# Products with low weights moved to the end of each projection's half in a hybrid decoder layer, with a new order of all work

## Chip, cores and metric

The kernel runs on one core of one Trainium2 chip. The metric is device time in microseconds for one call, the median of several runs. TensorE (PE) does the matrix products, VectorE (DVE) and ScalarE (ACT) the elementwise work, GpSimd (POOL) issues the accumulating transfers, and SyncE (SP) all other transfers.

## What is computed

One decoder layer for 1024 tokens of width 1024, all in float32. Attention (16 query heads, 4 key heads, head size 64) mixes three dilated windows; beside it stands a causal convolution over 31 tokens, followed by a layer norm. Both branches are gated, and one output projection brings them together.

```python
h = rmsnorm(x, norm_g)
proj = einsum('bsd,de->bse', h, w_in)            # 1024 -> 5632 columns
q, k, v, a_gate, c_val, c_glu, c_gate = split(proj)
y_att = attention_branch(q, k, v, a_gate)        # windows (128,1) (512,4) (2048,16)
y_conv = conv_branch(c_val, c_glu, c_gate, conv_w, conv_b, ln_g, ln_b)
x = x + einsum('bse,ed->bsd', concat([y_att, y_conv]), w_out)
return rmsnorm(x, final_norm_g)
```

## The kernel before

**Products in pieces.** PE takes its operands in a rounded 32-bit form, so each float32 matrix is split into a high part (a rounded copy) and a low part (the rest), and a product A·W is three: high·high, low·high and high·low. For the in-projection (`inproj`, L637) the pieces are `hhi`, `hlo` (normed input, one pair per half of the tokens) and `wh`, `wl` (128 columns of the weights, loaded as `raw`). There are 44 such column blocks; each has two halves of 512 tokens, and each half takes 24 products in one PSUM bank, named `ps`. In this document a block is named by its first column: ps2304 is the block at column 2304, ps2304_0 its first half.

**Weights.** For 40 of the 44 blocks `split_dma` makes the pieces: SP loads `raw`, ACT writes `wh` and then minus `wh` into `wl`, and a transfer issued by POOL adds `raw` into `wl` (`add_into`, L297). So `wl` is complete one transfer later than `wh`. For the first two blocks and for those with the last gates DVE subtracts instead.

**Attention.** `attend(p)` handles one pair of heads (p = 0 to 7). It takes scores in units: six far units (two named far0, far1, far3 for each head), which use `qf` and cover the dilated windows, then a small round trip through DRAM, then eight near units (near0 to near6 for each head), which use `qs`. Each unit is a few small products on PE into one of two score banks, then one or more `add_min` on DVE (L283, it adds the bias table and takes the minimum) and an exponential on ACT (L251). A bank is free for the next unit but one only when DVE has read it. Then follow transposes (`tp`), products with the values (`on`, `of`), a transfer of the result to `y` by POOL, the gate on DVE (`y<-y,ag`, L268) and a store to `y_dram`. The query projection also writes `qs` by DVE (L268) and `qf` by ACT.

**Convolution.** `convolve(p)` is 46 multiply-adds on DVE per block (L268, buffers `c`, `t`, `hc`), which are spread over the same stretch as the attention of pair p.

**End.** After the last pair come a layer norm of the convolution's result in two halves (`cc`, `mean`, `var`, `lst`, `rb`: PE sums, DVE finishes, PE spreads `rb` over the partitions), the output projection of the attention (`opsa`, eight row blocks, low pieces of the input `yla`), and that of the convolution (`opsc`, low pieces `ylc`).

**Who sets the order.** The functions above only record operations in a `Plan`: engine, modelled cost, inputs and outputs. `Plan.order` then simulates all engines and picks for each the operation that can start first, with a priority that is the place in the recorded order less a boost (`TUNE`: `w` loads and splits of weights, `use` what reads a projection's bank, `ln`, `att`, `conv`, `ap` and `wo` the streams of that name). `LIMITS` caps how many buffers of a kind are alive at once, and `SECTIONS` lists which projections run beside which pair (`h4` is a convolution block's two projections, `q3` a query block, `a2` a gate). What comes out is pinned: each engine's instructions and each queue's transfers run strictly in that order. So one changed line in `inproj` or one changed number can move work everywhere.

Of the kernel before, what the change touches and what calls it, by code (L numbers as in the profile page):

```python
# [19 lines left out]
ND = D // P  # L20
# [11 lines left out]

LIMITS = {"x": 5, "raw": 2, "raw_oc": 1, "raw_oa": 2, "wh": 3, "wl": 3, "tab": 1, "e": 7, "pt": 4, "vs": 4, "vc":
          4, "turn": 2, "opsa": 2, "score": 2, "hc": 5, "c": 7, "t": 1, "g": 1, "gl": 7, "y": 2, "ag": 4, "cc": 5,
          "qs": 5, "qf": 4, "kdh": 9, "kdl": 5, "yc": 1, "ya": 2, "zc": 7, "za": 3}

RESERVE = {"e": 7, "pt": 3}
BANKS = {"mm": 3, "sc": 2, "tp": 2, "o": 1}  # L40
WARM = 55
LATE = C_CG + 6 * P
MORE = (10, 12)
TUNE = {"w": 225, "use": 260, "ln": 65, "att": 240, "conv": -15, "wo": 185, "woa": 20, "ap": 0, "wait": 0.2116}
SECTIONS = [("k0 q0 h1 v", 0), ("h2 a0 q1", 1), ("h3 a1 q2", 1), ("a2 q3 h4", 1), ("h5 k1 a3 q4", 1), ("h6 a4 q5",
            1), ("c0 h7 a5 q6 c1 q7", 1), ("a6 a7 c2 c3", 1), ("c4 c5", 1), ("c6 c7", 0)]


# [113 lines left out]
class Plan:  # L162
# [140 lines left out]
    def order(self):  # L303
# [55 lines left out]
        while len(out) < n:  # L359
            best = None  # L360
            for e, todo in ready.items():
                now, pick = None, None
                for i in sorted(todo, key=self.prio.__getitem__):
                    t = start_of(i)
                    if t is None:
                        continue
                    soon = t - TUNE["wait"] if self.prio[i] < i - 300 else t
                    if now is None or soon < now - 1e-9:
# [94 lines left out]
def layer_kernel(tc, x, norm_g, w_in, conv_w, conv_b, ln_g, ln_b, w_out, fin_g, tab, out):  # L463
# [3 lines left out]
    def pool(name, space=None):  # L467
# [4 lines left out]
    pl = Plan(tc, {  # L472
        "big": (sb, "big", 4), "c8": (sb, "c8", 1), "c4": (sb, "c4", 33), "c2": (sb, "c2", 5), "st": (sb, "st", 16),
        "sx": (sb, "sx", 6),
        **{k: (ps, k, BANKS[k]) for k in PSUM_KINDS},
    }, LIMITS)

# [34 lines left out]
    def c4(shape, name, dtype=F32):  # L512
        group = name.rstrip("0123456789_")
        return pl.buf("c4", shape, dtype, name, group=group if group in pl.limits else None)

    def bank(kind, name, group=None):
        return pl.buf(kind, [P, 512], F32, name, group=group)
# [24 lines left out]
    hhi = [pl.buf("big", [P, ND, 512], F32R, f"hhi{i}") for i in range(2)]  # L542
    hlo = [pl.buf("big", [P, ND, 512], F32R, f"hlo{i}") for i in range(2)]
# [9 lines left out]
    raw, ready = {}, {}  # L553
# [68 lines left out]
    def load_raw(col):  # L622
        raw = c4([P, ND, P], f"raw{col}")
        pl.load(raw, w_in[:, col:col + P].rearrange("(c p) n -> p c n", p=P))
        return raw

    def split_w(col, raw, split=split_dma):
        wh, wl = c4([P, ND, P], f"wh{col}", F32R), c4([P, ND, P], f"wl{col}", F32R)
        split(wh, wl, raw)
        return wh, wl  # L630

    def load_w(col):
        if col in ready:
            return ready[col]
        old, pl.boost = pl.boost, TUNE["w"]
        w = split_w(col, load_raw(col), split_r if col >= LATE else split_dma)
        pl.boost = old  # L637
        return w

    def inproj(col, use, cuts=((0, 512), (0, 512))):  # L640
        wh, wl = load_w(col)
        for half in range(2):
            b = bank("mm", f"ps{col}_{half}")
            for n0, n1 in zip(cuts[half], cuts[half][1:]):
                if n0:
                    yield 0.5
                for c in range(ND):
                    pl.mm([(b[:, n0:n1], wh[:, c, :], hhi[half][:, c, n0:n1], c == 0, False),
                           (b[:, n0:n1], wh[:, c, :], hlo[half][:, c, n0:n1], False, False),
                           (b[:, n0:n1], wl[:, c, :], hhi[half][:, c, n0:n1], False, c == ND - 1)])  # L650
            pl.boost = TUNE["use"]
            use(half, b, slice(half * 512, half * 512 + 512))
            pl.boost = 0
            yield 1.0
# [3 lines left out]
    vs = [c4([P, 2, NKV, P], f"vs{i}", F32R) for i in range(4)]  # L658
    vc = [c4([P, 2, NKV, P], f"vc{i}", F32R) for i in range(4)]
# [4 lines left out]
    def project_v():  # L664
        for n in range(2):
            vt, vn = c4([P, 4, 256], f"vt{n}"), c4([P, 8, 4, 32], f"vn{n}")

            def use(half, b, cs):
                pl.act(rest(vt, half), b.fourth(), AF.Copy)
                pl.act(vn[:, 4 * half:4 * half + 4], b.blocks(), AF.Copy)  # L670
            yield from inproj(C_V + n * P, use)
            for g in range(4):
                for name, to in (("n", vs), ("f", vc)):
                    b = bank("tp", f"vT{n}_{name}{g}")
                    src = [vn[:, i].flat() if name == "n" else vt[:, g, (i % 2) * P:(i % 2) * P + P]
                           for i in (2 * g, 2 * g + 1)]
                    pl.mm([(b[:, j * P:(j + 1) * P], src[j], ident, None, None) for j in range(2)])
                    both = to[g][:, :, 2 * n:2 * n + 2, :]
                    split_r(both[:, :, :, 0:DH], both[:, :, :, DH:P],
                            b[:, 0:256].shaped("p (j k d) -> p j k d", 2, 2, DH, j=2, k=2))  # L680
# [3 lines left out]
    def project_k(kc):  # L684
        for kv in (2 * kc, 2 * kc + 1):
            kd[kv] = (c4([P, 4, 256], f"kdh{kv}", F32R), c4([P, 4, 256], f"kdl{kv}", F32R))

        def use(half, b, cs):
            for j in range(2):
                kh, kl = kd[2 * kc + j]  # L690
                r, o = slice(j * DH, j * DH + DH), slice((1 - j) * DH, (1 - j) * DH + DH)
                h, l, src = rest(kh, half), rest(kl, half), b[r, :].fourth()
                pl.act(h[r], src, AF.Copy)
                pl.act(h[o], src, AF.Copy)
                pl.tt(l[r], src, h[r].cast(F32), ALU.subtract)
                pl.act(l[o], l[r].cast(F32), AF.Copy)
        yield from inproj(C_K + kc * P, use)

    qs, qf = {}, {}

    def project_q(p):
        for j in range(2):
            qs[2 * p + j] = c4([P, S], f"qs{2 * p + j}", F32R)
            qf[2 * p + j] = c4([P, 2, 4, P], f"qf{2 * p + j}", F32R)

        def use(half, b, cs):
            for j in range(2):
                q = qs[2 * p + j]
                r, o = slice(j * DH, j * DH + DH), slice((1 - j) * DH, (1 - j) * DH + DH)
                pl.act(q[r, cs], b[r, :], AF.Copy, scale=-(DH ** -0.5))  # L710
                pl.stt(q[o, cs], b[r, :], -(DH ** -0.5), q[r, cs].cast(F32), ALU.mult, ALU.subtract)
                pl.act(qf[2 * p + j][:, half], q[:, cs].fourth().cast(F32), AF.Copy)
        yield from inproj(C_Q + p * P, use)
# [6 lines left out]
    ag = {}  # L720
# [15 lines left out]
    hc = {}  # L736
# [361 lines left out]
    def boosted(name, gen):  # L1098
        while True:
            pl.boost = TUNE[name]  # L1100
            w = next(gen, None)
            pl.boost = 0
            if w is None:
                return
            yield w

    def section(k, weight, spine, more=()):
        nonlocal done
        proj, m = SECTIONS[k]
        hs = [boosted("att", attend(i)) for i in range(done, done + m)]  # L1110
# [48 lines left out]
```

## Time and profile before

| | us |
|---|---|
| median of 3 runs (909.42 to 910.8) | 910.27 |
| the profiled execution's own time | 910.03 |
| its span, first to last instruction | 908.2 |
| PE busy | 875.1 (96%) |
| DVE busy | 656.1 (72%) |
| ACT busy | 591.3 (65%) |
| POOL busy | 53.3 (6%) |

The span is what the trace covers; 1.8 us of the profiled execution's time lie around it. Three views are used below. The view of waits lists how long an engine stood before an instruction and what it stood for. The view of windows gives, for a stretch of time, each engine's busy time and PEclk, the share of full speed that the TensorE clock was granted. The timeline gives single instructions with their start.

### The profile page before, as it was taken

How to read it: one execution, taken by the hardware profiler on the slowest of the kernel's cores; microseconds unless marked ns; L12 is line 12 of the kernel's file. 1: busy time of each engine (PE TensorE's matmuls, PEld its weight loads, DVE VectorE, ACT ScalarE, POOL GpSimd, SP SyncE). 2: the span in 40 equal slices, each digit the busy share in tenths (PEclk: the TensorE clock that was granted, in tenths of full speed). 3: DMA queues.
4: the chain of work that ended last, by engine and by line, in shares of the span. 5: the costliest groups of instructions: out<-in, count | busy, mean ns of one | idle time of the engine just before them, and what ended most of it. 6: DMA issues, size and time to landing. Idle time of an engine off the chain costs nothing. (4 is left out here: it accounts for less than half of the span.)

```text
span 908.2 us, 13036 instructions
## 1 busy us (share of the span) xinstructions
PE 875.1 (96%) x4493; PEld 731.2 (81%) x4493; DVE 656.1 (72%) x1506; ACT 591.3 (65%) x1392; POOL 53.3 (6%) x69
## 2 busy tenths in 40 slices
PE   8999999999999999999998998899999899999996
PEld 7888888878888888878886887688887678778885
DVE  5769995798699699989587658874659895615432
ACT  5777469387979889678786764795796754404111
POOL 0011001101010110100011000001000000000000
PEclk9999999999999999999999999699999999999999
DMA  7653306436353673464357323366765697758211
GB/s 259 186 119 67 96 3 140 93 91 144 70 118 59 163 165 83 93 135 101 96 128 173 70 70 92 73 152 132 206 201 194 186 372 255 252 177 239 93 47 47
DMA packets 104953, 123.53 MB, mean 136 GB/s; under 512 B 17941, under 2 KB 78357, under 8 KB 104888
## 3 DMA queue, kind: packets, MB, share of 16 engines
q1 hardware_dynamic: 97000, 94.40, 33.6%
q0 software_dynamic: 7888, 28.32, 17.2%
q8 instruction: 35, 0.57, 0.3%
q14 instruction: 30, 0.25, 0.1%
HBM read 65.35 MB, written 24.84 MB: 99 GB/s over the span
## 5 line engine op out<-in xcount | busy, mean ns | idle before, releaser
L236 PE MATMUL ps<-hhi,wh 128*128 128x512 f32 (+1 forms) x720 | 291.1, 404 | 0.2 <-ACT hhi L249 0.2
L236 PE MATMUL ps<-hhi,wl 128*128 128x512 f32 (+1 forms) x720 | 282.3, 392 | 6.1 <-DMA wl<-raw 4.8
L236 PE MATMUL ps<-hlo,wh 128*128 128x512 f32 (+1 forms) x720 | 281.8, 391 | 0.4 <-DVE hlo L264 0.3
L236 PEld LDWEIGHTS ps<-hhi,wl 128*128 128x128 f32 x720 | 136.6, 190 | 38.2 <-DMA wl<-raw 6.5
L236 PEld LDWEIGHTS ps<-hlo,wh 128*128 128x128 f32 x720 | 137.2, 191 | 23.8 <-DVE hlo L264 1.0
L236 PEld LDWEIGHTS ps<-hhi,wh 128*128 128x128 f32 x720 | 137.0, 190 | 23.0 <-issue 0.5
L251 ACT ACTIVATE e<-e,near 128x256 f32<-128x256 f32 (+1 forms) x256 | 115.0, 489 | 17.4 <-DVE near L264 11.5
L268 DVE SCALAR_TENSOR_TENSOR c<-t,taps,c 128x511 f32<-128x511 f32 (+14 forms) x120 | 88.5, 737 | 0.0
L268 DVE SCALAR_TENSOR_TENSOR c<-hc,taps,c 128x511 f32<-128x511 f32 (+14 forms) x120 | 88.2, 735 | 0.3
L268 DVE SCALAR_TENSOR_TENSOR t<-hc,taps,t 128x511 f32<-128x511 f32 (+6 forms) x112 | 82.6, 738 | 0.3 <-ACT t L251 0.2
L236 PE MATMUL opsc<-woc,yhc 128*128 128x512 f32 (+1 forms) x272 | 81.0, 381 | 0.0
L251 ACT ACTIVATE e<-e,far 128x96 f32<-128x96 f32 (+1 forms) x128 | 53.8, 423 | 25.9 <-DVE far L283 25.2
L297 POOL DMA_DIRECT2D wl<-raw x40 | 34.9, 873 | 414.2 <-ACT wl L251 315.5
L236 PEld LDWEIGHTS opsc<-woc,yhc 128*128 128x128 f32 x272 | 50.1, 188 | 10.7
L236 PE MATMUL opsc<-woc,ylc 128*128 128x512 f32 (+1 forms) x136 | 52.0, 383 | 1.4 <-DVE ylc L264 1.4
L251 ACT ACTIVATE fjunk<-zc 128x512 bf16<-128x512 f32 (+1 forms) x17 | 10.3, 606 | 62.2 <-DVE zc L264 62.2
L236 PE MATMUL opsa<-woah,yla 128*128 128x512 f32 x112 | 45.0, 402 | 2.6 <-DVE yla L264 2.6
L249 ACT CAST wh<-raw 128x1024 fp32r<-128x1024 f32 x44 | 46.0, 1046 | 0.4 <-DMA raw<-in_w_in 0.4
L236 PE MATMUL opsa<-woah,yha 128*128 128x512 f32 x112 | 45.6, 408 | 0.4 <-DVE cc L264 0.4
L236 PE MATMUL opsa<-woal,yha 128*128 128x512 f32 x112 | 45.1, 402 | 0.0
L251 ACT ACTIVATE e<-e,f 128x224 f32<-128x224 f32 (+1 forms) x128 | 45.0, 436 | 0.0
L249 ACT CAST qf<-qs 128x512 fp32r<-128x512 f32 x32 | 34.3, 1120 | 13.5 <-DVE qs L268 13.5
(176 smaller groups left out, 1525.2 us busy)
## 6 DMA issues: line engine op xcount, KB each, us to landing
raw<-in_w_in SPq DMA_DIRECT2D x44, 512.0 KB, 5.4
wl<-raw POOLq DMA_DIRECT2D x40, 512.0 KB, 4.7
x<-in_x SPq DMA_DIRECT2D x8, 512.0 KB, 10.2
tab<-in_tab SPq DMA_DIRECT2D x8, 512.0 KB, 3.8
c_dram<-c SPq DMA_DIRECT2D x8, 512.0 KB, 2.7
g_dram<-g SPq DMA_DIRECT2D x8, 512.0 KB, 3.1
raw_oa<-in_w_out SPq DMA_DIRECT2D x8, 512.0 KB, 5.1
raw_oc<-in_w_out SPq DMA_DIRECT2D x8, 512.0 KB, 7.9
```

The source lines that it names most:

```text
L236: nc.tensor.matmul(out.ap(), a.ap(), b.ap(), start=start, stop=stop)
L249: nc.scalar.copy(out.ap(), x.ap())
L251: nc.scalar.activation(out.ap(), x.ap(), func, **{k: ap_of(v) for k, v in kw.items()})
L268: lambda: self.nc.vector.scalar_tensor_tensor(out.ap(), a.ap(), ap_of(s), b.ap(), op0, op1),
L297: self.op("POOL", 1.0, lambda: self.nc.gpsimd.dma_start(ap_of(dst), x.ap(), accum_op=ALU.add), [dst], [x, dst])
```

## The change

In `inproj` the 24 products of a half are issued in another order. Before: eight times (high input with high weights, low input with high weights, high input with low weights). Now: eight times the first two, 16 products in all, then the 8 products with low weights in four operations of two. The products are the same and their number too. The buffer limits (`wl`, `hc`, `c`, `gl` and `za` one more; `y`, `qs` and `kdh` one fewer), six boosts, and the place of the gate projection `a2` change with it, and the order of all engines comes out anew.

```diff
--- before.py
+++ after.py
@@ -32,17 +32,17 @@
 
 
 
-LIMITS = {"x": 5, "raw": 2, "raw_oc": 1, "raw_oa": 2, "wh": 3, "wl": 3, "tab": 1, "e": 7, "pt": 4, "vs": 4, "vc":
-          4, "turn": 2, "opsa": 2, "score": 2, "hc": 5, "c": 7, "t": 1, "g": 1, "gl": 7, "y": 2, "ag": 4, "cc": 5,
-          "qs": 5, "qf": 4, "kdh": 9, "kdl": 5, "yc": 1, "ya": 2, "zc": 7, "za": 3}
+LIMITS = {"x": 5, "raw": 2, "raw_oc": 1, "raw_oa": 2, "wh": 3, "wl": 4, "tab": 1, "e": 7, "pt": 4, "vs": 4, "vc":
+          4, "turn": 2, "opsa": 2, "score": 2, "hc": 6, "c": 8, "t": 1, "g": 1, "gl": 8, "y": 1, "ag": 4, "cc": 5,
+          "qs": 4, "qf": 4, "kdh": 8, "kdl": 5, "yc": 1, "ya": 2, "zc": 7, "za": 4}
 
 RESERVE = {"e": 7, "pt": 3}
 BANKS = {"mm": 3, "sc": 2, "tp": 2, "o": 1}
 WARM = 55
 LATE = C_CG + 6 * P
 MORE = (10, 12)
-TUNE = {"w": 225, "use": 260, "ln": 65, "att": 240, "conv": -15, "wo": 185, "woa": 20, "ap": 0, "wait": 0.2116}
-SECTIONS = [("k0 q0 h1 v", 0), ("h2 a0 q1", 1), ("h3 a1 q2", 1), ("a2 q3 h4", 1), ("h5 k1 a3 q4", 1), ("h6 a4 q5",
+TUNE = {"w": 255, "use": 150, "ln": 205, "att": 240, "conv": -75, "wo": 195, "woa": 20, "ap": 180, "wait": 0.2116}
+SECTIONS = [("k0 q0 h1 v", 0), ("h2 a0 q1", 1), ("h3 a1 q2 a2", 1), ("h4 q3", 1), ("h5 k1 a3 q4", 1), ("h6 a4 q5",
             1), ("c0 h7 a5 q6 c1 q7", 1), ("a6 a7 c2 c3", 1), ("c4 c5", 1), ("c6 c7", 0)]
 
 
@@ -646,8 +646,10 @@
                     yield 0.5
                 for c in range(ND):
                     pl.mm([(b[:, n0:n1], wh[:, c, :], hhi[half][:, c, n0:n1], c == 0, False),
-                           (b[:, n0:n1], wh[:, c, :], hlo[half][:, c, n0:n1], False, False),
-                           (b[:, n0:n1], wl[:, c, :], hhi[half][:, c, n0:n1], False, c == ND - 1)])
+                           (b[:, n0:n1], wh[:, c, :], hlo[half][:, c, n0:n1], False, False)])
+                for c in range(0, ND, 2):
+                    pl.mm([(b[:, n0:n1], wl[:, c + i, :], hhi[half][:, c + i, n0:n1], False, c + i == ND - 1)
+                           for i in range(2)])
             pl.boost = TUNE["use"]
             use(half, b, slice(half * 512, half * 512 + 512))
             pl.boost = 0
```

Three places of the new order follow. The first is PE's queue in pair 6, from the end of projection ps896 (`ps_1_5562` here; ps2304 is `ps_0_5703`) over the far scores of the pair's second head to its near scores. Before:

```order
L236 MATMUL ps_1_5562<-hhi_424,wl_5275 128x512
L236 MATMUL sc_1far_5613<-kdh_3677,qf_5355 128x96
...
L236 MATMUL sc_1far_5622<-kdh_3677,qf_5355 128x224
...
L236 MATMUL sc_1far_5634<-kdh_3677,qf_5355 128x224
...
L236 MATMUL sc_0near_5647<-kdh_3677,qs_5318 128x128
...
L236 MATMUL sc_1near_5694<-kdh_3677,qs_5326 128x128
...
L236 MATMUL ps_0_5703<-hhi_234,wh_5631 128x512
```

After (ps2304 is `ps_0_5596` and `ps_1_5641`):

```order
L236 MATMUL ps_1_5557<-hhi_455,wl_5136 128x512 x8
L236 MATMUL ps_0_5596<-hhi_234,wh_5536 128x512
...
L236 MATMUL sc_1far_5627<-kdh_3615,qf_5327 128x96
...
L236 MATMUL sc_1far_5636<-kdh_3615,qf_5327 128x224
...
L236 MATMUL ps_1_5641<-hhi_455,wh_5536 128x512
...
L236 MATMUL sc_1far_5659<-kdh_3615,qf_5327 128x224
...
L236 MATMUL sc_0near_5682<-kdh_3615,qs_5296 128x128
...
L236 MATMUL ps_0_5596<-hhi_234,wl_5646 128x512 x2
```

Before, all of the far and near units of this stretch up to the first near unit of the second head stand one behind the other, and ps2304 begins after them. Now 16 products of ps2304's first half stand ahead of them and more of the second half between them; the products with `wl` come later, between the near units.

The second place is SP's queue before projections ps4480 and ps3456, whose weights are `raw_4547` and `raw_4825` before and `raw_4748` and `raw_4784` after. Before:

```order
L300 DMA c_dram<-c_3905 128x1024
L294 DMA raw_4547<-in_w_in 128x8x128
L300 DMA y_4708<-comb_4391 64x1024 x2
L300 DMA y_dram<-y_4708 128x1024
L294 DMA raw_4825<-in_w_in 128x8x128
L300 DMA there_93<-far_4672 128x32
```

After:

```order
L300 DMA c_dram<-c_3817 128x1024
L300 DMA y_4710<-comb_4406 64x1024 x2
L300 DMA y_dram<-y_4710 128x1024
L294 DMA raw_4748<-in_w_in 128x8x128
L294 DMA raw_4784<-in_w_in 128x8x128
L300 DMA g_dram<-g_4760 128x1024
```

Before, the weights of ps4480 are loaded ahead of the store of the fifth pair's `y`, which waits for DVE's gate; now both loads stand behind that store.

The third place is DVE's queue in the second half of the layer norm (`lst` and `rb`). The low pieces for row blocks 5 and 6 of the attention's output projection are `yla_7494` and `yla_7547` before, `yla_7359` and `yla_7441` after. Before:

```order
L274 TENSOR_SCALAR lst_7396<-var_7384 128x4
...
L268 SCALAR_TENSOR_TENSOR lst_7396<-lst_7396 128x4 x2
...
L264 TENSOR_TENSOR cc_0_6909<-cc_0_6909,rb_7420 128x512 x2
...
L264 TENSOR_TENSOR cc_3_7211<-cc_3_7211,rb_7420 128x512 x2
...
L264 TENSOR_TENSOR yla_7494<-ya_7290,yha_7380 128x896
...
L264 TENSOR_TENSOR yla_7547<-ya_7394,yha_7522 128x896
```

After:

```order
L264 TENSOR_TENSOR yla_7359<-ya_7268,yha_7343 128x896
...
L264 TENSOR_TENSOR yla_7441<-ya_7380,yha_7419 128x896
L264 TENSOR_TENSOR za_7328<-opsa_512_7415,za_7328 128x512
L274 TENSOR_SCALAR lst_7465<-var_7453 128x4
...
L268 SCALAR_TENSOR_TENSOR lst_7465<-lst_7465 128x4 x2
L264 TENSOR_TENSOR cc_0_6915<-cc_0_6915,rb_7485 128x512 x2
...
L264 TENSOR_TENSOR cc_3_7181<-cc_3_7181,rb_7485 128x512 x2
```

Before, both of them stand behind the layer norm's `lst` and `rb` work; now both stand ahead of it.

## Rows read from the trace of the kernel before

**Rows 1.** The page: the span, and busy time by engine.
```profile
span 908.2 us, 13036 instructions
PE 875.1 (96%) x4493; PEld 731.2 (81%) x4493; DVE 656.1 (72%) x1506; ACT 591.3 (65%) x1392; POOL 53.3 (6%) x69
```

**Rows 2.** Waits of PE, by line: total us, times, longest us.
```profile
PE ps L236 <- DMA wl<-raw: 4.8, 4, 4.1
PE sc_1far L236 <- DVE far L283: 4.5, 1, 4.5
PE opsa L236 <- DVE yla L264: 2.6, 2, 2.2
PE sc_0near L236 <- DVE near L283: 2.5, 3, 1.0
PE rb L236 <- DVE lst L268: 2.3, 1, 2.3
PE sc_0far L236 <- ACT qf L249: 2.1, 2, 1.1
PE sc_0near L236 <- DVE far L283: 2.0, 2, 1.2
...
PE opsc L236 <- DVE ylc L264: 1.4, 1, 1.4
PE ps L236 <- DVE wl L264: 1.3, 1, 1.3
```

**Rows 3.** Windows: stretch, length, busy us by engine (PE PEld DVE ACT POOL), PEclk, DMA, GB/s.
```profile
14.00:24.00 10.00, 8.08 (x53) 7.44 (x50) 7.85 (x15) 6.43 (x13) 0.00 (x0) 0.83 0.60 177
24.00:150.00 126.00, 125.79 (x661) 105.48 (x661) 106.62 (x244) 88.61 (x212) 9.67 (x11) 1.00 0.43 101
480.00:497.00 17.00, 12.94 (x53) 10.31 (x53) 13.99 (x36) 11.62 (x27) 2.56 (x3) 0.90 0.77 168
562.00:584.00 22.00, 14.81 (x65) 12.49 (x64) 18.06 (x60) 15.20 (x49) 0.89 (x1) 0.69 0.44 104
706.00:724.00 18.00, 15.34 (x66) 11.99 (x65) 15.89 (x29) 13.88 (x20) 0.00 (x0) 0.91 0.66 208
770.00:785.00 15.00, 12.82 (x49) 9.96 (x48) 14.33 (x23) 11.89 (x18) 0.00 (x0) 0.89 0.75 253
```

**Rows 4.** Timeline of PE: start us, duration us, instruction, idle time before it.
```profile
487.65 0.39 PE L236 MATMUL ps<-hhi,wh 128*128 128x512 f32 x1
487.88 0.40 PE L236 MATMUL ps<-hlo,wh 128*128 128x512 f32 x1
...
492.34 0.50 PE L236 MATMUL ps<-hhi,wl 128*128 128x512 f32 x1 [4.06 <-DMA wl<-raw]
...
564.37 0.28 PE L236 MATMUL sc_1far<-kdl,qf 128*128 128x224 f32 x1
569.14 0.56 PE L236 MATMUL sc_1far<-kdh,qf 128*128 128x224 f32 x1 [4.49 <-DVE far L283]
```

**Rows 5.** Timeline of DVE, around 180 us and 565 us.
```profile
179.92 1.23 DVE L268 SCALAR_TENSOR_TENSOR y<-y,ag 128x1024 f32<-128x1024 f32 x1 [2.21 <-DMA y<-comb]
...
564.06 1.23 DVE L268 SCALAR_TENSOR_TENSOR y<-y,ag 128x1024 f32<-128x1024 f32 x1 [0.86 <-DMA y<-comb]
...
565.98 1.41 DVE L268 SCALAR_TENSOR_TENSOR qs<-ps,qs 64x512 fp32r<-64x512 f32 x2
```

**Rows 6.** Timeline of POOL, the low weights of one projection.
```profile
483.33 0.85 POOL L297 DMA_DIRECT2D wl<-raw  x1 [13.67 <-ACT wl L251]
```

**Rows 7.** DMA issues: count, KB each, median us from issue to landing.
```profile
wl<-raw POOLq DMA_DIRECT2D x40, 512.0 KB, 4.7
...
cc<-c_dram SPq DMA_DIRECT2D x8, 512.0 KB, 7.0
```

**Rows 8.** Groups of DVE instructions by line and shape: busy us, mean ns.
```profile
L283 DVE CUSTOM_DVE_ANT_0 e<-sc_0near,tab 128x256 f32<-128x256 f32 x56 | 21.3, 420 | 1.4 <-PE sc_0near L236 1.4
```
## The prediction, made before the changed kernel ran

> **What bounds the kernel now.** I read four views. The page comes first: PE is busy for 875.1 of 908.2 us, DVE for 656.1 [rows 1], so PE sets the time and only what holds PE up can be won. The second view is PE's waits: the nine lines shown sum to 23.5 us, and none is one broad cause [rows 2]. The third is the windows, for the clock. In an even stretch such as 24 to 150 us, PE is busy for 125.79 of 126 us at PEclk 1.00, the level of 2.4 GHz. Five short stretches lie below it [rows 3]. With only the levels 1.2 and 2.4 GHz, a mean of c over a length L means 2·(1−c)·L at the lower one: 3.4 us in 14 to 24, 3.4 in 480 to 497, 13.6 in 562 to 584, 3.2 in 706 to 724, 3.3 in 770 to 785. A product there takes twice as long, so up to half of that is lost: 1.7, 1.7, 6.8, 1.6 and 1.65, together 13.5 us. Each of the last four stretches holds a PE wait of over 2 us (4.1, 4.5, 2.3 and 2.2) [rows 2, 3], so a long wait costs itself and then some clock. All waits and lost clock together are 37 us: more than that this change can't win on PE. Last come the timelines, for the place of each wait. There, the pace of products of 512 columns is 0.23 us, from start to start [rows 4].
>
> **The change, part by part.** Work on PE is the same: no product is added or dropped, so at 0.23 us each the 2112 in-projection products cost what they did. The gains are covers: 16 products with high weights run before the first with low weights, so `wl` is wanted 16·0.23 = 3.7 us later counted from the half's start.
>
> *Head.* The first projection waits 1.3 us for `wl`, which DVE makes [rows 2]. The 16 products, of 256 columns here, cover it. I take the wait and half of the 1.7 us of clock: **−2.2** (ends −3.0 and 0).
>
> *Scores of pairs 1 to 3.* At 180 us DVE stands 2.21 us before `y<-y,ag`, for POOL's transfer, and the query's `qs` is queued behind it [rows 5]; PE waits for `qf`, which needs `qs`. In the new DVE order the `qs` pair stands ahead of y0. One of the two `qf` waits goes (1.0 of 2.1); in pair 4 the same pattern stays. Pair 2's and pair 3's near scores get projection products between them: the longest near-after-far wait (1.2) and the longest near-after-near (1.0) go [rows 2]. **−3.2** (ends −6.6, all three lines, and 0).
>
> *ps3456.* POOL issues its `wl` at 483.33 and PE uses it at 492.34, 9.0 us later, having stood 4.06 us [rows 4, 6]; the median from issue to landing is 4.7 [rows 7]. Being wanted 3.7 us later covers all but 0.4, and the 1.7 of clock come back: −5.4. Against it, SP's queue now has the weights of ps4480 and ps3456 both behind the store of the fifth `y`, and that store waits for DVE's gate, which waits for POOL's transfer. The wait in front of that gate was 2.21 and 0.86 where I show it [rows 5], so I add 2.4, the upper one and a little: **−3** (ends −5.8 and +1). The Trainium skill, "DMA: Bandwidth & Descriptors", section on the anatomy of one DMA on the GpSimd path, gives 2.0 us plus the bytes at 436 GB/s, which is by my estimate 3.2 us for 512 KB. The trace disagrees, with 4.7 as the median and 9.0 here; by the page the low weights would arrive with no wait left and this term would be −5.8.
>
> *Pair 6, the largest.* In 562 to 584 PE is busy for 14.81 of 22 us, so idle 7.2 [rows 3]; 4.49 of it is one wait at 569.14 for DVE's read of a far score [rows 4]. DVE was then at y<-y,ag from 564.06 and at two `qs` from 565.98 [rows 5], and PE had nothing but scores in its queue. If all the idle time falls in the 13.6 us at the lower level, 6.4 us of work ran there and lost 3.2; at most it is 6.8. The cluster costs 10.4 to 14.0, I take 12. In the new order 16 products of ps2304 (3.7 us) stand ahead of these units and 14 more (3.2 us) between them up to the first near unit: 6.9 us against 7.2 idle. What is late next is the near units of the second head; I leave 0.5 us: **−11.5** (ends −14 and −7, the latter if `wh` of ps2304 is itself late from ACT and the clock falls again).
>
> *Layer norm, first half.* PE's `rb` waits 2.3 us for `lst` and the clock loses 1.6 [rows 2, 3]. Now 30 projection products stand between `var` and `rb`, so 3.9 goes. But `mean` comes about 30 products (7 us) earlier in PE's order, and the first `cc` load now reuses a buffer which pair 7's first `on` group gives free. `cc` takes 7.0 from issue to landing [rows 7], DVE stands for it with pair 7's transposes behind, and `raw_oa` loads wait for a later buffer. Between 0 and 7.0 I take the middle, 3.9 when rounded up: **0** (ends −3.9 and +3.1).
>
> *Layer norm, second half.* `yla` for row blocks 5 and 6 now stands ahead of the `lst`, `rb` work on DVE, so the wait of 2.2 and its 1.65 of clock go [rows 2, 3]: **−3.9** (ends −3.9 and 0, if the rotation makes `yla` 7 late instead).
>
> *Last part.* The first low piece for `opsc` still follows the last `opsa` sum on DVE: its wait of 1.4 stays [rows 2]. From there on the order is as before: 0.
>
> *Waits that I don't see.* Every queue is new, and the SP, ACT and POOL orders shift with it (one `y` buffer in place of two makes the `y` transfers follow each other). A new order has its own short waits. The nearest rows are the short score waits, 6.6 us over the whole old order [rows 2]; I take **+5** (ends 0 and +10).
>
> The sum: −2.2 −3.2 −3 −11.5 +0 −3.9 +5 = −18.8 against the profiled execution's own 910.03, so 891.2; the median of the runs stands 0.24 above that execution, and I forecast **891 us**. About 0.2%, 1.8 us, is what a measurement of this kernel can tell from no change.
>
> **Rivals.**
>
> *New waits eat most of it.* The late `raw` loads of ps4480, the `cc` loads and the unseen waits come at their upper ends: −2.2 −3.2 +1 −11.5 +3.1 −3.9 +10 = −6.7, 903.5 us. For it: the long landing of 9.0 in a busy stretch [rows 4, 6]. Against: PE has more independent products between scores than before.
>
> *Only the direct effect.* The `wl` waits go, all else comes back in other places: −1.3 −0.85 −4.8 −1.7 = −8.7, 901.5 us. For it: the waits of rows 2 are scattered, as if any order had its share. Against: pair 6's cluster has one visible cause, which is gone.
>
> *Slower: DVE falls behind in the near units.* Projection work can now fill the space between two score units in steps of two products, 0.46 us, where it was three, 0.69. Each unit asks two reads of 0.42 us of DVE [rows 8] besides the convolution. If all 64 near units come 0.23 us short, that is 14.7 us, and if each pair then drops the clock once for 1.7 us, 13.6 more: 891 + 28 = 919 us. It decides from the point where 14.7 us are joined by three clock drops (the gain of 19 is then gone). For it: DVE was busy for 18.06 of 22 us where PE stood longest [rows 3]. Against: from 24 to 150 us DVE is busy for 106.62 of 126 us and PE never stands [rows 3], and a planner that counts DVE's time puts more products where units are late. The Trainium skill, "TensorE: Matmul & The Clock Gate", section on a second failure mode, says that brief, frequent idling between groups of products can make the clock swing without any long gap. In the stretches with a lowered clock shown here there is always a wait of 1.3 us or more, so the trace doesn't bear that out so far; by it this rival would be the likelier.
>
> *The change does nothing:* the wait for `wl` becomes one for `wh` or `raw`, since the same loads bound both, and the tuned numbers only shift waits. 909 to 911 us. Against: ACT's `wh` copy precedes `wl` by a whole transfer.
>
> **How the numbers follow.** My forecast 0.55 (own range 884 to 898, from −26 to −12), new waits 0.17, direct effect only 0.13, slower 0.09, nothing 0.06. The range 881 to 905 takes in the first three and leaves out the last two. Faster 0.85, same 0.06, slower 0.09.
>
> **What would show it.** Right: the line of `ps` waiting for `wl` under 1.5 us in total, no line of `sc_1far` waiting for DVE over 2 us, no wait of `opsa` for `yla` over 1 us, PE's span less its busy time down from 33 to about 20 us, and mean PEclk of 0.98 or more in every stretch of 20 us after the first. Wrong: a wait for `raw` or `wh` near ps4480, `cc` or `rb` waits over 3 us around the layer norm, many `sc` near waits, or a stretch below 0.8.

## The result, and the profile after

The changed kernel takes 900.25 us, median of 4 runs (897.05 to 901.16), against 910.53 for the kernel before (909.42 to 910.95). The ratio is 0.988, with a 95% interval of 0.986 to 0.991: faster by 10 us, or 1.2%, with no overlap of the two ranges, where 19 us were forecast. The profiled execution took 901.16 us, with a span of 899.4; it is the slowest of the four.

The page, as in [rows 1]:

```profile
span 899.4 us, 13058 instructions
PE 868.5 (97%) x4493; PEld 727.2 (81%) x4493; DVE 655.7 (73%) x1506; ACT 591.2 (66%) x1392; POOL 53.3 (6%) x69
```

PE is busy for 6.6 us less with the same instructions, and idle for 30.9 us (899.4 − 868.5) where it was 33.1. So most of the 8.8 us between the spans came as a higher clock, and only 2.2 us as less idle time. PE's waits show why:

```profile
PE sc_1far L236 <- DVE far L283: 8.2, 2, 7.2
PE sc_0near L236 <- DVE far L283: 4.0, 1, 4.0
...
PE sc_0far L236 <- ACT qf L249: 1.4, 2, 1.1
PE opsa L236 <- DVE g L268: 1.3, 1, 1.3
PE ps L236 <- ACT wh L249: 1.1, 2, 0.6
...
PE opsa L236 <- DVE yla L264: 0.2, 1, 0.2
```

The lines of [rows 2] that the prediction wanted gone are gone or small: no `ps` waits for `wl`, none for `rb`, `opsa` waits 0.2 us for `yla`, the score waits for `qf` are down to 1.4. But scores wait 8.2 and 4.0 us for DVE, more than the largest line before. The windows, with columns as in [rows 3], show where:

```profile
14.00:24.00 10.00, 8.82 (x71) 8.06 (x70) 8.26 (x16) 6.29 (x12) 0.00 (x0) 1.00 0.63 178
320.00:331.00 11.00, 7.05 (x33) 5.58 (x32) 6.39 (x21) 5.25 (x19) 1.97 (x3) 0.91 0.86 187
331.00:350.00 19.00, 19.00 (x89) 16.20 (x89) 17.00 (x56) 14.57 (x42) 2.58 (x3) 0.87 0.62 140
480.00:497.00 17.00, 16.86 (x87) 14.21 (x86) 17.00 (x50) 11.18 (x34) 0.85 (x1) 1.00 0.64 161
560.00:584.00 24.00, 22.89 (x119) 18.73 (x118) 21.92 (x72) 20.43 (x57) 2.08 (x3) 1.00 0.59 134
634.00:650.00 16.00, 8.82 (x43) 7.65 (x42) 6.04 (x31) 6.47 (x26) 0.02 (x1) 0.79 0.93 247
690.00:708.00 18.00, 18.00 (x86) 14.09 (x84) 17.21 (x28) 14.23 (x19) 0.00 (x0) 1.00 0.61 198
756.00:776.00 20.00, 20.00 (x97) 16.56 (x96) 10.56 (x20) 9.33 (x13) 0.00 (x0) 1.00 0.64 201
```

The five stretches that answer to the lowered ones of [rows 3] all stand at PEclk 1.00 now: 14 to 24, 480 to 497, 560 to 584 (the pair 6 cluster, PE busy for 22.89 of 24 us), 690 to 708 and 756 to 776 (the two halves of the layer norm). In their place are two new holes, one in 320 to 331 us and one in 634 to 650 us, and as long as PE has work the clock is lower only in and behind these two.

DVE's timeline shows what stood there. Columns are start, duration, instruction and the idle time before it:

```profile
328.93 1.23 DVE L268 SCALAR_TENSOR_TENSOR y<-y,ag 128x1024 f32<-128x1024 f32 x1 [4.61 <-DMA y<-comb]
330.07 0.25 DVE L283 CUSTOM_DVE_ANT_0 e<-sc_1far,tab 128x96 f32<-128x96 f32 x1
...
639.94 1.23 DVE L268 SCALAR_TENSOR_TENSOR y<-y,ag 128x1024 f32<-128x1024 f32 x1 [7.25 <-DMA y<-comb]
641.08 0.25 DVE L283 CUSTOM_DVE_ANT_0 e<-sc_1far,tab 128x96 f32<-128x96 f32 x1
```

Both are the gate `y<-y,ag`: y2 at 328.93, after 4.61 us of standing, and y6 at 639.94, after 7.25, each for POOL's transfer into `y`. Reads of far scores are next in DVE's queue. On PE, the first near scores of pair 3 and the far scores of pair 7 wait for one of those reads to free a score bank:

```profile
330.39 0.48 PE L236 MATMUL sc_0near<-kdh,qs 128*128 128x128 f32 x1 [3.95 <-DVE far L283]
...
634.12 0.40 PE L236 MATMUL ps<-hlo,wh 128*128 128x512 f32 x1
641.70 0.56 PE L236 MATMUL sc_1far<-kdh,qf 128*128 128x224 f32 x1 [7.18 <-DVE far L283]
```

The products ahead of the wait of 7.18 are the last with high weights of ps5120; those with low weights stand behind it in PE's queue.

A long wait of the gate is not new. In the kernel before, the gate y6 stood nearly 5 us, and it cost PE nothing: PE is busy for all of 626 to 642 us there, and no score is read behind the gate before 641.38, when DVE waits for PE and not PE for DVE. Rows of DVE, and the window:

```profile
635.71 1.23 DVE L268 SCALAR_TENSOR_TENSOR y<-y,ag 128x1024 f32<-128x1024 f32 x1 [4.96 <-DMA y<-comb]
...
641.38 0.26 DVE L283 CUSTOM_DVE_ANT_0 e<-sc_1far,tab 128x96 f32<-128x96 f32 x1 [3.85 <-PE sc_1far L236]
```

```profile
626.00:642.00 16.00, 16.00 (x78) 13.26 (x77) 3.12 (x6) 6.01 (x11) 3.40 (x4) 1.00 0.90 192
```

What is new for y6 is that far scores are taken ahead of the gate, their reads stand behind it, and PE can't go on without these.

To see what each stage gained, I added up the undisturbed start-to-start times of PE's list (0.231 us for a product of 512 columns, 0.118 for 224 to 256, 0.109 for a transpose, 0.08 for smaller products, and so on), and took from each start in the trace the sum of everything ahead of it. Both lists sum to 847.3 us. How much that delay grows in a stage of before and of after is what the stage loses to waits and clock (with plain medians as unit times, single differences move by up to 0.5 us):

| stage (us in the trace before) | before | after | measured | forecast |
|---|---|---|---|---|
| head, to 50 | 9.1 | 7.3 | −1.8 | −2.2 |
| scores of pairs 1 and 2, to 283 | 7.2 | 4.7 | −2.5 | −3.2 |
| pair 3, to 393 (gate y2) | 1.2 | 8.3 | +7.1 | |
| pairs 4 and 5, ps3456, to 512 | 9.4 | 3.8 | −5.6 | −3 |
| pair 6, to 636 | 14.1 | 5.9 | −8.2 | −11.5 |
| pair 7, to 691 (gate y6) | 0.2 | 10.1 | +9.9 | |
| layer norm, first half, to 764 | 6.1 | 2.3 | −3.8 | 0 |
| second half and the rest | 6.1 | 2.3 | −3.8 | −3.9 |
| waits not seen | | | | +5 |
| sum | 53.4 | 44.7 | −8.7 | −18.8 |

The spans differ by 8.8. The six stages that the prediction named give −25.7, where it had −23.8. The two unseen ones cost 17, where it had 5.

### The profile page after: what moved, and what is told of

It is laid out like the page before. It is cut to its first block, busy times and chain, and to the rows that moved or that the text cites. A ratio compares the mean times of both kernels' runs of the same rounds, so it can differ in the third digit from the quotient of the medians.

```text
span 899.4 us, 13058 instructions
## 1 busy us (share of the span) xinstructions
PE 868.5 (97%) x4493; PEld 727.2 (81%) x4493; DVE 655.7 (73%) x1506; ACT 591.2 (66%) x1392; POOL 53.3 (6%) x69
## 4 chain that ended last, share of the span: by engine, by line
PE 70%; DVE 10%; DMA 9%; ACT 7%; issue 2%; SPq 1%; POOL 0%; DVEq 0%; ACTq 0%; POOLq 0%
PE ps L236 38%; PE opsc L236 10%; PE opsa L236 9%; DMA y<-comb 5%; ACT e L251 3%; PE on L236 2%; PE sc_0near L236 2%; DVE c L268 2%; PE sc_1near L236 2%; PE of L236 2%; SPq L294 1%; ACT pt L249 1%; DVE comb L264 1%; PE sc_1far L236 1%; PE tp_m L234 1%
## 5 line engine op out<-in xcount | busy, mean ns | idle before, releaser
L236 PE MATMUL ps<-hhi,wh 128*128 128x512 f32 (+1 forms) x720 | 285.4, 398 | 1.3 <-ACT wh L249 1.1
L236 PE MATMUL ps<-hhi,wl 128*128 128x512 f32 (+1 forms) x720 | 189.8, 396 | 0.0
L236 PEld LDWEIGHTS ps<-hhi,wl 128*128 128x128 f32 x720 | 129.9, 190 | 25.5 <-DMA wl<-raw 0.6
L251 ACT ACTIVATE e<-e,near 128x256 f32<-128x256 f32 (+1 forms) x256 | 115.7, 489 | 18.7 <-DVE near L264 11.5
```

The source lines that it names most:

```text
L236: nc.tensor.matmul(out.ap(), a.ap(), b.ap(), start=start, stop=stop)
L251: nc.scalar.activation(out.ap(), x.ap(), func, **{k: ap_of(v) for k, v in kw.items()})
```

## The experiments

The theory after this result: the change's covers work as forecast, and two gates on DVE, y2 and y6, give most of the gain back, since far reads are queued behind a gate that waits for a transfer. The rivals: DVE simply has too much work in those stretches, so that a wait would only move on; or the gain is that of the products alone, and the new order adds nothing.

**Products alone, in the old order.** The plan is made with the old products, so every queue is as before; only what PE issues in the 24 places of a half is permuted. In short:

```diff
+ new = [(b, wh[c], x[half][c]) for c in range(ND) for x in (hhi, hlo)]
+ new += [(b, wl[c], hhi[half][c]) for c in range(ND)]
  for c in range(ND):
-     pl.mm([hhi*wh, hlo*wh, hhi*wl])
+     pl.mm([hhi*wh, hlo*wh, hhi*wl], emit=new[3 * c:3 * c + 3])
```

> The old order of all engines, each half's 24 products permuted in their own places on PE (high weights first, low weights last). If the direct effect of the change is only that low weights are wanted later: the waits for wl (4.8 + 1.3 us) and their clock go, all other waits of the old order stay: 900 to 903 us, against 910.5 before. If the gain of the change came from the products alone: about 900 with sc_1far and opsa waits shortened too. If the waits only move to wh: 909 to 911.

Measured: 901.96 us (898.99 to 903.57), ratio 0.989 (0.986 to 0.993). Its waits, and its window at ps3456:

```profile
PE sc_1far L236 <- DVE far L283: 4.5, 1, 4.5
...
PE opsa L236 <- DVE yla L264: 2.2, 1, 2.2
...
PE ps L236 <- DMA wl<-raw: 1.2, 1, 1.2
```

```profile
480.00:497.00 17.00, 15.76 (x76) 12.85 (x75) 16.14 (x40) 13.33 (x32) 2.56 (x3) 1.00 0.81 179
```

The wait for `wl` is down from 4.8 to 1.2 and the clock in 480 to 497 is back at 1.00, while the waits for `far` and `yla`, and the 2.3 of `rb`, are what they were in [rows 2]. This is the direct effect as the second rival of the prediction priced it, 901.5, and it is nearly as large as the whole change's net gain. So the new order's further gains and its two new holes nearly cancel.

**Numbers alone, products alone with a new plan.** The first takes the old products with the new limits, boosts and sections, the second the new products with the old ones; both are planned anew. The first in short:

```diff
- LIMITS, TUNE, SECTIONS as before
+ LIMITS, TUNE, SECTIONS as in the change
```

> The old products with the new limits, boosts and sections; the order is computed anew. If the tuned numbers alone repair the old order's waits: 900 to 905 us. If they fit only the new products: 908 or more, with waits for wl of 4 us and more in the list.

Measured: 925.44 us (924.84 to 928.1), ratio 1.017 (1.014 to 1.020). Its largest waits:

```profile
PE sc_0far L236 <- ACT qf L249: 6.7, 3, 3.1
PE ps L236 <- DMA wl<-raw: 5.8, 5, 3.3
```

> The new products with the old numbers; the order is computed anew. If the cover by products with high weights is what removes waits: 898 to 904 us, without a wait for wl. If the numbers are needed: 906 or more, with a long wait of scores for DVE.

Measured: 916.51 us (911.81 to 923.83), ratio 1.008 (1.005 to 1.011). The profiled execution took 923.4, near the upper end, so its waits are longer than those of the median. The largest:

```profile
PE opsa L236 <- DVE yla L264: 9.4, 1, 9.4
PE sc_0near L236 <- DVE far L283: 6.4, 3, 4.5
PE opsa L236 <- DVE cc L264: 4.9, 1, 4.9
```

Neither half alone gives a gain once the order is planned anew. The second has no long wait for `wl`, as expected, and two of its three largest waits stand at the end (`opsa` for `yla` 9.4 us, for `cc` 4.9). Its expectation of a cover that suffices fell. The same two parts that give 916 and 925 apart give 900 together, so what a new plan brings depends on which waits it happens to make. That can be 15 us: the same products take 901.96 in the old order and 916.51 in a new one, and the old products 925.44 in a new order against some 910.

**Gates later.** The changed kernel, its order pinned, with single operations moved in the list before it is issued. A gate and the store that needs it go behind a named read of the next pair; `sc3_0near2` is that of the units near2 of pair 3's first head.

```diff
+ LATER = [("gate2", "sc3_0near2"), ("gate6", "sc7_0near2")]
```

> The changed kernel with one move: on DVE the gates y2 and y6 (and on SP their stores) stand after the second near score's read of the next pair instead of among its far reads; all else pinned. If far reads queued behind a gate that waits for POOL's transfer are what is left (7.2 + 4.0 us of PE waits, some 3 to 4 us of clock): 887 to 891 us, no sc_1far wait over 1 us. If DVE has too much work there, or the transfers hold up something else too, the wait moves on to the near scores: 897 to 901 us.

Measured: 889.03 us (887.28 to 894.18), ratio 0.977 (0.973 to 0.981). The wait did not move on to the near scores. One `sc_1far` wait of 1.7 us is left, over the 1 us that was expected, in pair 2, where the gate y1 was not moved. DVE has the time; what it lacked was something other than the gate at the front of its queue.

```diff
+ LATER = [("gate6", "sc7_0near2")]
```

> The changed kernel with only the gate y6 moved on DVE. If the two long waits add up independently (7.2 + about 2 us of clock for y6; 4.0 + 2.7 for y2): 893 to 895 us. If the first one alone carried most of the gain of the two: 889 to 891.

Measured: 892.58 us (891.43 to 895.09), just below the 893 to 895 of two waits that add up. So y6 is worth 7.7 us and y2 another 3.5, together the 11.2 of the two. The 3.5 is rough, as the ranges of the two runs overlap, and it is well below the 6.7 that the expectation gave y2. The table had 9.9 and 7.1 for the whole stages, so these keep some loss of their own.

**All gates later.**

```diff
+ LATER += [("gate0", "sc1_1far3"), ("gate1", "sc2_0near0"), ("gate3", "sc4_1far3"),
+           ("gate4", "sc5_1far3"), ("gate5", "sc6_0near2")]
```

> The changed kernel with all seven gates y0 to y6 moved behind far or near reads of the next pair on DVE, their stores likewise on SP; all else pinned. If every gate that stands ahead of score reads costs its transfer's rest: the waits of 1 to 2 us left at pairs 2 and 4 go too, 884 to 887 us. If only the two long ones mattered: 888 to 890, as with two gates moved. If later stores and buffers bring new waits: over 891.

Measured: 893.3 us (890.37 to 896.29). The median is 4 us above that with two gates, but the ranges overlap. Its largest waits:

```profile
PE sc_1near L236 <- DVE near L283: 4.3, 5, 1.5
PE sc_0near L236 <- DVE near L283: 1.9, 3, 0.8
```

With two gates moved, y0, y4 and y5 stood for 1.5, 1.9 and 0 us, and PE had no wait for a score in these places beyond 0.6 us. Now no gate waits at all, but each of these three does its 1.23 us of work among reads that PE needs, and the waits for near scores sum to 6.2 us where they were 1.9. That this is what cost the gain is likely, not shown. With y1, y2, y3 and y6 moved, and y0, y4 and y5 left where they were:

> The changed kernel with the gates y1, y2, y3 and y6 moved, y0, y4, y5 left in place. If the moved y0, y4 and y5 brought the near score waits of the run with all seven: 886 to 889 us. If any gate moved without a long wait costs what it saves: 889 to 893.

Measured: 888.82 us (887.49 to 890.95), no different from two gates, and within the 886 to 889 of the first case. The profiled execution, the slowest of the four with 890.95, has one long near wait all the same, and it isn't from y0, y4 or y5. The gate y6 in its new place still stood for 3.06 us, and a near score waited behind it:

```profile
634.54 1.23 DVE L268 SCALAR_TENSOR_TENSOR y<-y,ag 128x1024 f32<-128x1024 f32 x1 [3.06 <-DMA y<-comb]
```

```profile
636.60 0.30 PE L236 MATMUL sc_1near<-kdh,qs 128*128 128x128 f32 x1 [3.92 <-DVE near L283]
```

So a later gate is a cure only as long as the transfer has landed by then.

**The transfer itself.** POOL issues its adds into y6 at 630.99, 9 us after SP's copies into the same buffer. SP's queue and POOL's in the changed kernel:

```profile
619.14 0.40 SPq L294 DMA_DIRECT2D raw<-in_w_in  x1
622.00 1.11 SPq L300 DMA_DIRECT2D y<-comb  x2
...
632.66 0.69 SPq L294 DMA_DIRECT2D raw<-in_w_in  x1
633.45 1.35 SPq L294 DMA_DIRECT2D raw_oa<-in_w_out  x1
```

```profile
630.99 1.69 POOL L297 DMA_DIRECT2D y<-comb  x2 [12.31 <-DVE far L283]
```

The list puts POOL's wait of 12.31 us down to a read of far scores on DVE that ended just before. It was the copies: in the run with three loads moved (below) the same add goes out at 626.09, and DVE does this read only at 630.83. A store (618.70) and a load of 512 KB each run just ahead of the copies, two loads run beside the adds. First only the two later ones were moved behind the store of y6:

```diff
  y6<-comb (SP), y6<-comb (POOL)
- raw5376 load, raw_oa0 load
  y_dram<-y6
+ raw5376 load, raw_oa0 load
```

> The changed kernel; on SP the loads raw5376 and raw_oa0 (512 KB each) stand behind the store of y6, so that they no longer run beside POOL's transfer into y6. If that transfer is long (8.2 us from issue to landing) because it shares the DMA engines with them: it lands in 6 us or less, the PE wait of 7.2 us falls to 5 or less, 896 to 898 us. If its length is its own: landing 8 us, the wait stays at 7, 900 us.

Measured: 898.05 us (894.38 to 898.93), ratio 0.985 (0.983 to 0.988). The adds go out from 630.52 and the gate starts at 638.27, 7.8 us later where it was 9.0, and `sc_1far` waits 5.7 us at most instead of 7.2:

```profile
638.27 1.23 DVE L268 SCALAR_TENSOR_TENSOR y<-y,ag 128x1024 f32<-128x1024 f32 x1 [5.85 <-DMA y<-comb]
```

The waits came out between the two cases: these loads are a small part. The time of 2 us less isn't clear of the ranges, which overlap. Then the load ahead of the copies too:

```diff
- raw5248 load
  y6<-comb (SP)
+ raw5248 load
```

> The changed kernel; on SP the load raw5248 stands behind the two copies into y6 instead of ahead of them, and raw5376 and raw_oa0 behind the store of y6; DVE's order is untouched. If the copies into y6 come late (8 us from issue to POOL's add) because 512 KB of weights run ahead of them: POOL's add starts 3 us sooner, DVE stands at the gate of y6 for 3 us or less instead of 5.9 to 7.3, and sc_1far waits for 2 us or less: 892 to 895 us. If the copies' time is their own: the wait stays at 5.7, 898 us.

Measured: 892.48 us (892.13 to 893.67), ratio 0.980 (0.977 to 0.982). SP's copies, POOL's adds and DVE's gate in this kernel:

```profile
622.50 1.12 SPq L300 DMA_DIRECT2D y<-comb  x2
623.71 0.57 SPq L294 DMA_DIRECT2D raw<-in_w_in  x1
```

```profile
626.09 0.85 POOL L297 DMA_DIRECT2D y<-comb  x1 [6.90 <-DVE g L268]
```

```profile
633.05 0.08 DVE L283 DVE_READ_ACCUMULATOR2_ANT far<- 128x1 f32 x1
633.05 1.22 DVE L268 SCALAR_TENSOR_TENSOR y<-y,ag 128x1024 f32<-128x1024 f32 x1
```

POOL's first add follows the copies by 3.6 us instead of 9.0, and the gate does not wait at all, with DVE's queue untouched. That is the same 8 us as moving the gate away. The long wait needs both: a transfer that is late, and reads that PE needs queued behind what waits for it. For y2 only the move of the gate was tried, not its transfer.

**The old order's cluster.** Was the cluster of before also a gate? In the old order with permuted products, only y5's gate was moved behind near reads:

> The old order with the products permuted in place, and only the gate y5 moved behind the second near read of pair 6. If the old cluster at 562 to 584 us came mainly from the gate and its wait (0.86 + 1.23 us ahead of the far reads): 890 to 894 us. If the gate is one of several DVE steps there, as the prediction had it (two qs and the convolution too): 897 to 900. If PE lacks other work anyway: 902, unchanged.

Measured: 902.47 us (900.39 to 905.14), no gain over 901.96. The PE wait there is shorter, 3.1 us where it was 4.5, and the near units behind it wait as before:

```profile
561.66 0.55 PE L236 MATMUL sc_1far<-kdh,qf 128*128 128x224 f32 x1 [3.09 <-DVE far L283]
```

> The old order with the products permuted in place and the gates y0, y1, y3 to y6 moved behind far or near reads. If gates explain the old order's score waits: 888 to 893 us with no score wait over 1.5 us. If the lack of projection products between the scores does: 896 to 900, and a wait of sc_1far in pair 6 stays above 2 us.

Measured: 901.57 us (899.08 to 902.98), above the 896 to 900 of the case without products, though its sign, a wait of `sc_1far` over 2 us in pair 6, is there with 3.1. The old cluster isn't the gates': with them gone, PE still has only scores in its queue there and waits for DVE's `qs` and far reads. That fits the prediction's cause, the lack of other products. In the changed kernel DVE goes through the same steps (`qs` at 564.49, the gate at 566.60, far reads from 567.85), but PE is busy with 16 products of ps2304 up to 566.80. No run takes only these products out, so that they removed the cluster is likely, not shown.

**Both cures.** The three loads moved for y6, and the gates y1, y2 and y3 moved:

> The changed kernel with the three loads moved behind y6's transfers and store (as in the run before), y6's gate in its place, and the gates y1, y2, y3 moved on DVE. If what a gate costs is the rest of its transfer, an early transfer and a late gate are two cures of the same wait and add up over different places: 885 to 888 us, no PE wait above 2 us. If they disturb each other: 889 or more, with a near score wait of 3 us or more.

Measured: 887.71 us (886.27 to 891.02), ratio 0.975 (0.971 to 0.979), the lowest median of the study; it can't be told from 888.82 and 889.03, so that the two cures add up is not shown by the time. No wait of scores is over 0.9 us:

```profile
PE sc_1far L236 <- DVE far L283: 0.9, 1, 0.9
```

## Why the prediction came out as it did

The direction held, and so did the stated range of 881 to 905. The time was 900 where 891 was forecast, at about half of the gain, and so outside the forecast's own range of 884 to 898: the wider range held because it took in two rivals. Of the five signs of being right two came (no wait of `ps` for `wl`, 0.2 us of `opsa` for `yla`). Three did not: `sc_1far` waits 8.2 us for DVE, PE is idle for 30.9 us and not 20, and PEclk is 0.87 in 331 to 350 and 0.79 in 634 to 650. The last is also one of the signs of being wrong, a stretch below 0.8. The covers were understood; what a new order brings with it was not.

- *Head, −2.2, and scores of pairs 1 to 3, −3.2*: −1.8 and, for pairs 1 and 2, −2.5. Of the right size. The second `qf` wait of 1.1 in pair 4 stayed, as said.
- *ps3456, −3*: −5.6. The 2.4 us set aside for weights queued behind the store of y4 were too much: ps4480 starts with a delay of 0.8. The sum without that charge, −5.4, would have been right.
- *Pair 6, −11.5*: −8.2. The cluster is gone as forecast. The runs in the old order show that the gates were not its cause and fit the one named, without isolating it. The new order has short waits of its own in that stage.
- *Layer norm, first half, 0*: −3.8. The charge of 3.9 for `cc` loads and their followers did not come; only a wait of 1.3 before the first `opsa` did.
- *Layer norm, second half, −3.9*: −3.8.
- *Waits that I don't see, +5*: +17. This is the step that failed, outside its upper end of 10. It was sized by the short score waits of before. The right rows were in the trace: the gate's own wait, as a charge wherever reads of scores stand behind a gate. I used it once, for the weights of ps3456, and never for the far reads of pairs 3 and 7, though the new order's DVE queue shows the gates y2 and y6 among them. I also took it too small: 2.21 is the larger of the two in [rows 5], but the view of DVE's waits of the kernel before has one of 5.0, which is y6 at 635.71, so a charge at y6 of 5 us and its clock could have been read off. One at y2 could not: this gate stood for nothing there.
- *The rivals.* Of the three costs in "new waits eat most of it" two stayed away, the late weights of ps4480 and the `cc` loads; the third, the unseen waits, was 17 where it had 10. "Only the direct effect" gave the right price for the products, 901.5 against 901.96, but the wrong reason for the total: the other waits went, and new ones came. That the total also lies near 901.5 is chance. "Slower: DVE falls behind in the near units" did not happen; PE waits 0.6 us for a near read in the changed kernel. With that rival stood the Trainium skill, "TensorE: Matmul & The Clock Gate", section on a second failure mode, with brief idling as enough to make the clock swing. The trace after does not bear it out: the stretches without a long wait stand at 1.00, and the lower ones follow waits of 4.0 and 7.2 us.

What stays open: why SP's copies into y6 take as long as they do behind one store and one load. That moving the load of 512 KB behind them shortens the step from the copies to the add is shown; how the transfers share the DMA engines is not. In the changed kernel the DMA share falls from 0.92 in 626 to 628 us to 0.03 in 629 to 631, and the add still goes out only at 630.99; what held up this small rest is not known. Why y2's transfer was late was not tried.

## What to carry to other kernels

On an engine that runs strictly in order, an operation that waits for a transfer is a charge on everything behind it: list what it waits for, when that lands at the worst in the trace, and who waits for what is queued behind. Either pull the transfer ahead of other large ones or put the waiting operation behind the work that feeds the critical engine, but leave those alone behind which the critical engine doesn't wait: moving y0, y4 and y5 too brought no gain. And when a change makes a planner lay out everything anew, separate the two: pin the old order and make the edit alone, to see what is the edit's and what is the layout's.

## What the runs showed of the hardware

How long a transfer takes depends much on what else is under way. From the issue of the copies into y6 to POOL's add behind them it took 9.0 us in the changed kernel, with 512 KB of weights issued 2.9 us ahead of the copies, and 3.6 us with the same load issued behind them. Other runs have the same two orders: with the load ahead 8.7 and 8.9 us (the two later loads moved; four gates moved) and 6.8 to 6.9 us (two gates, one gate, all gates moved), with the load behind 4.9 us (both cures). Each is one profile. So the load ahead costs 2 to 5 us, with a wide spread. The Trainium skill, "DMA: Bandwidth & Descriptors", section "Issuing engines are not separate DMA queues", says that transfers started by different engines run on the same 16 DMA engines and interleave. The trace fits: from POOL's adds into y6 to the gate it took 9.0 us with two loads of SP's beside them, and 7.8 with these loads moved away.
